# Second mixer's end: all weight subtractions of the output projection on VectorE, and the last two head pairs' softmax scaling too

## The chip, the cores and the metric

The kernel runs on one core of a Trainium2 chip. The time is the device time of one execution in microseconds (us); what is compared is the median of several runs. The engines run side by side, each through its own list of instructions in order: TensorE (PE in the profile, its weight loads PEld) multiplies, VectorE (DVE), ScalarE (ACT) and GpSimd (POOL) do the elementwise work, and SyncE's queue (SP) issues the loads of weights. Engines wait for each other by semaphores.

## The reference, cut to what matters

A decoder trunk of two layers on 256 tokens of width 1024, in float32. Each layer is a half-weighted feed-forward block (SwiGLU, inner width 2816), a token mixer, and a second feed-forward block; the first layer's mixer is a gated DeltaNet, the second layer's is attention in a sliding window with a learned sink per head. The change lies in that second mixer:

```python
def mixer_sliding_window_sinks(h, w_in, b_in, sinks, w_out, b_out):
    ...
    proj = h @ w_in + b_in
    ...
    s = jnp.einsum("bnqhgd,bnkhd->bnhgqk", q, kk).astype(jnp.float32) * (B_HD ** -0.5)
    ...
    p = jax.nn.softmax(jnp.concatenate([s, sink], axis=-1), axis=-1)[..., :-1]
    o = jnp.einsum("bnhgqk,bnkhd->bnqhgd", p.astype(vv.dtype), vv)
    return o.reshape(Bsz, T, HQ) @ w_out + b_out
```

There are 16 query heads of width 64 and 4 key/value heads. The output projection `w_out` is 1024 x 1024.

## The kernel before

**Split operands.** To keep float32's precision on TensorE, each operand is split into a rounded part and a remainder. A weight piece of 512 KB is loaded by SP into a `raw` tile (four buffers), rounded to `whi` by a ScalarE cast (L296), and its remainder `wlo = raw - whi` is made by a subtraction (L297) on VectorE, or on GpSimd where the caller names that engine. A product is then three multiplications (L341 to L343: high x high, high x remainder, remainder x high). A `raw` buffer is free for the next load when its subtraction is done.

**The second mixer, `swa`.** The heads are worked in eight pairs, numbered 0 to 7, each by a generator `attend(j)` whose steps are spread between other work. For a pair TensorE makes the scores (L1152: `psp`, `psc`), VectorE masks them and takes the row maximum (L1162 to L1171), ScalarE takes the exponentials with their row sums (L1176), VectorE adds the sink and takes the reciprocal (L1178, L1179), and one engine multiplies the weights with it (L1180, `att<-att,sl`). After that TensorE transposes them (L1186, `ppt`); ScalarE copies the first token block's part (L1188) and VectorE masks the second's (L1189). The value products follow (L1196, `po`): two for the first token block, which need the copy of L1188, and four for the second, which need L1189. Last, ScalarE casts the result to `oTh` (L1200) and VectorE makes the remainder `oTl` (L1201).

**The output projection.** `out_weights` (L477) loads eight pieces of `w_out`, numbered 0 to 7 here; piece k belongs to pair k. `out` adds a pair's contribution to four accumulators `acc`, in the gaps that `attend` leaves (the list `fill`). In the program's own numbers pieces 4 and 5 are `whi2_8172`/`wlo2_8173`, 6 and 7 are `whi2_8182`/`wlo2_8183`; pair 5's weights are `att_8125`, pair 6's `att_8208`, pair 7's `att_8257`. `po_8241` is pair 4's result, `po_8298` pair 5's, `po_8332` pair 6's. Behind the mixer follows the second feed-forward block, whose first three weight pieces are `raw_8475`, `raw_8482` and `raw_8489`; each is issued by SP as two DMAs of 256 KB (L286), as soon as a `raw` buffer is free, so while the mixer still runs.

**What sets the order.** The kernel is written in one sequence, but the framework's scheduler plans the order on each engine, with its own estimates of durations; a few places are tied by hand with `issue_after`. So a moved instruction shifts its neighbours' places too. Before the change pieces 4 and 6 are subtracted by GpSimd, and all eight pairs' multiplications at L1180 are GpSimd's.

Of the kernel before, what the change touches and what calls it, by code (L numbers as in the profile page):

```python
# [205 lines left out]
class Kern:  # L206
# [894 lines left out]
    def swa(self, nrm, prep, w_in, w_out, after):  # L1101
        nc = self.nc
        bcol, bv, sk, bo = prep
        NP = BH // 2
# [39 lines left out]
        def attend(j):  # L1144
            kv = j // 2
            at = self.big([P, 2048], "att")
            pr = at[:, 0:512].rearrange("p (b h k) -> p b h k", b=NT, h=2)
            pT = at[:, 512:1280].rearrange("p (n h q) -> p n h q", n=3, h=2)
            prv = pr.rearrange("p b h k -> p (b h) k")

            def score(out, b, kt):
                nc.tensor.matmul(out, lhsT=qT[:, j, b * P:(b + 1) * P], rhs=kz[:, kv, :, kt * P:(kt + 1) * P],  # L1152
                                 start=True, stop=True)

            psc, psp = self.psB("psc"), self.psB("psp")
            sc = psc.rearrange("p (b h k) -> p b h k", b=NT, h=2)
            sp = psp[:, 0:256].rearrange("p (h k) -> p h k", h=2)
            score(sp, 1, 0)
            score(sc[:, 1], 1, 1)
            score(sc[:, 0], 0, 0)  # L1160

            nc.vector.copy_predicated(sc[:, 1], self.gt.bitcast(mybir.dt.int32).unsqueeze(1).to_broadcast([P, 2, P]), sp)  # L1162
            nc.vector.tensor_tensor(out=sc[:, 0], in0=sc[:, 0], in1=self.neg.unsqueeze(1).to_broadcast([P, 2, P]),
                                    op=ALU.add)
            m = self.small([P, NT, 2], "smx", 4)
            nc.vector.tensor_reduce(out=m, in_=sc, axis=AX.X, op=ALU.max)
            skb = sk[:, 2 * j:2 * j + 2].unsqueeze(1).to_broadcast([P, NT, 2])
            nc.vector.scalar_tensor_tensor(out=m, in0=m, scalar=HD ** -0.5, in1=skb, op0=ALU.mult, op1=ALU.max)
            es = self.small([P, NT, 2], "ses", 4)
            nc.vector.tensor_tensor(out=es, in0=skb, in1=m, op=ALU.subtract)  # L1170
            nc.vector.tensor_scalar_mul(m, m, -1.0)  # L1171
            nc.scalar.activation(es, es, AF.Exp)
            l = self.small([P, NT, 2], "sl", 4)
            for b in range(NT):
                for i in range(2):
                    nc.scalar.activation(pr[:, b, i, :], sc[:, b, i, :], AF.Exp, scale=HD ** -0.5, bias=m[:, b, i:i + 1],  # L1176
                                         accum_out=l[:, b, i:i + 1])
            nc.vector.tensor_add(l, l, es)  # L1178
            nc.vector.reciprocal(l, l)  # L1179
            nc.gpsimd.tensor_tensor(  # L1180
                out=pr, in0=pr, in1=l.unsqueeze(3).to_broadcast([P, NT, 2, P]), op=ALU.mult)
            yield
            yield
            ps = self.psA("ppt")
            for n in range(4):
                nc.tensor.transpose(ps[:, n * P:(n + 1) * P], prv[:, n, :], self.ident)  # L1186
            pv = ps.rearrange("p (b h q) -> p b h q", b=NT, h=2)
            nc.scalar.copy(pT[:, 0], pv[:, 0])  # L1188
            nc.vector.tensor_tensor(out=pT[:, 1:3], in0=pv[:, 1:2].to_broadcast([P, 2, 2, P]),  # L1189
                                    in1=self.M["st"].unsqueeze(2).to_broadcast([P, 2, 2, P]), op=ALU.mult)  # L1190
            yield
            po = self.psA("po")
            for b in range(NT):
                for i in range(2):
                    for kt in range(b + 1):
                        lastpo[0] = nc.tensor.matmul(po[64 * i:64 * i + 64, b * P:(b + 1) * P],  # L1196
                                         lhsT=v[:, kt, kv * HD:(kv + 1) * HD], rhs=pT[:, b + kt, i, :],
                                         start=kt == 0, stop=kt == b)
            oh = oT_h[:, j, :]
            nc.scalar.copy(oh, po[:, :T])  # L1200
            nc.vector.tensor_sub(oT_l[:, j, :], po[:, :T], oh.bitcast(F32))  # L1201

        lastpo = [None]
        tk.add(attend(0))
        for c in range(1, 4):
            w = self.wcols(w_in, c * 256)
            for f in range(2):
                j = 2 * c + f
                ps = self.psA("pq")
                self.proj_T(ps[:, :T], w, f, nrm)  # L1210
                nc.scalar.activation(qT[:, j, :], ps[:, :T], AF.Identity, bias=bcol[:, j:j + 1])
                tk.tick()
                tk.add(attend(j - 1))
        ws = self.out_weights(w_out, (4, 6))
        tk.tick()
        tk.add(attend(NP - 1))
        oT = [(oT_h[:, :, t * P:(t + 1) * P], oT_l[:, :, t * P:(t + 1) * P]) for t in range(NT)]
        acc = [[ps("acc") for n in range(2)] for ps in (self.psA, self.psB)]
# [109 lines left out]
```

## Time and profile before

| what | value |
|---|---|
| median of 3 runs | 1031.77 us (1029.7 to 1032.34) |
| the profiled execution's own time | 1030.34 us |
| its span, first to last instruction | 1028.6 us |
| mean granted TensorE clock | 0.993 of full speed |
| busy share PE, DVE, ACT, POOL | 98%, 63%, 54%, 24% |
| second mixer's scores to its last value product | 771.7 to 827.5 us of the span |

Times within the span count from its first instruction. A busy share is an average over stages with different limits: what bounds one stage is read from its own stretch of the timeline. In a timeline, a row gives the start, the length, the engine, the line, what it writes and reads, and in brackets the idle time before it and who ended it; neighbouring equal instructions are merged.

### The profile page before, as it was taken

What the parts mean: (1) busy time and instruction counts of PE and PEld (TensorE: products, weight loads), DVE (VectorE), ACT (ScalarE), POOL (GpSimd) and SP (SyncE); (2) the same over time, 40 slices, a digit from 0 to 9 for tenths busy, and PEclk for the clock granted to TensorE, in tenths of its full rate; (3) what the DMA queues carried; (4) which work ended last, traced back from release to release, by engine and by line L of the source; (5) the groups of instructions that cost most, each with busy time, mean ns of one, the idle gap of its engine ahead of it and who ended that gap; (6) DMA issues with size and microseconds to landing.
All of it is one profiled execution on the core that took longest, in us unless ns stands there. A gap on an engine that the chain in (4) does not pass through costs nothing.

```text
span 1028.6 us, 16500 instructions
## 1 busy us (share of the span) xinstructions
PE 1003.0 (98%) x6211; PEld 873.3 (85%) x6211; DVE 649.5 (63%) x967; ACT 552.5 (54%) x1007; POOL 244.8 (24%) x277
## 2 busy tenths in 40 slices
PE   8999999999979999999999999999999999999997
PEld 6888888899878888888888888888898678888886
DVE  6866654666896766666645666664567756666544
ACT  7556543457755646555434555554366645555432
POOL 2233610006744201322200032330021401323100
PEclk9999999999989999999999999999999999999999
DMA  7666666644443335666665666666653426666661
GB/s 250 202 190 186 192 198 196 187 149 127 129 150 90 122 104 164 194 187 193 198 192 182 189 200 187 184 204 193 203 188 120 136 90 205 195 188 192 200 189 42
DMA packets 135252, 177.05 MB, mean 172 GB/s; under 512 B 7186, under 2 KB 120196, under 8 KB 135172
## 3 DMA queue, kind: packets, MB, share of 16 engines
q1 hardware_dynamic: 131968, 171.46, 54.9%
q10 hardware_dynamic: 3204, 4.53, 1.5%
q8 instruction: 49, 0.80, 0.3%
q14 instruction: 31, 0.25, 0.1%
HBM read 174.92 MB, written 1.05 MB: 171 GB/s over the span
## 4 chain that ended last, share of the span: by engine, by line
PE 62%; issue 1%; DVE 1%; ACT 1%; POOLq 0%; POOL 0%; ACTq 0%
PE pg L348 11%; PE pu L348 11%; PE acc L343 7%; PE acc L341 7%; PE acc L342 7%; PE pu L349 6%; PE pg L349 6%; PE pgu L343 1%; PE pgu L342 1%; PE pgu L341 1%; PE pq L341 1%; PE pq L343 1%; PE pq L342 1%; PE psc L1152 1%; PE po L1196 1%
## 5 line engine op out<-in xcount | busy, mean ns | idle before, releaser
L297 DVE TENSOR_TENSOR wlo<-raw,whi 128x1024 fp32r<-128x1024 f32 x302 | 379.9, 1260 | 202.7 <-ACT whi L296 201.7
L296 ACT CAST whi<-raw 128x1024 fp32r<-128x1024 f32 x316 | 330.3, 1052 | 184.8 <-PE acc L343 84.2
L348 PE MATMUL pg<-hs,whi 128*128 128x512 f32 x640 | 225.6, 394 | 0.3 <-DVE hs L203 0.3
L348 PE MATMUL pu<-hs,whi 128*128 128x512 f32 x640 | 225.1, 393 | 0.0
L349 PE MATMUL pu<-hs,wlo 128*128 128x256 f32 x640 | 179.7, 281 | 0.3 <-DVE wlo L297 0.3
L349 PE MATMUL pg<-hs,wlo 128*128 128x256 f32 x640 | 178.9, 280 | 0.0
L348 PEld LDWEIGHTS pg<-hs,whi 128*128 128x128 f32 x640 | 119.9, 187 | 27.7 <-DVE hs L203 0.7
L348 PEld LDWEIGHTS pu<-hs,whi 128*128 128x128 f32 x640 | 119.8, 187 | 27.0
L435 POOL TENSOR_TENSOR act<-act,gate 128x256 f32<-128x256 f32 x80 | 60.2, 752 | 346.5 <-DVE act L434 337.7
L342 PE MATMUL acc<-wlo,ah 128*128 128x512 f32 (+1 forms) x340 | 128.4, 378 | 0.0
L343 PE MATMUL acc<-whi,al 128*128 128x512 f32 (+1 forms) x340 | 128.2, 377 | 0.0
L341 PE MATMUL acc<-whi,ah 128*128 128x512 f32 (+1 forms) x340 | 127.8, 378 | 0.0
L349 PEld LDWEIGHTS pu<-hs,wlo 128*128 128x128 f32 x640 | 120.9, 189 | 0.6 <-DVE wlo L297 0.6
L349 PEld LDWEIGHTS pg<-hs,wlo 128*128 128x128 f32 x640 | 120.9, 189 | 0.4
L341 PEld LDWEIGHTS acc<-whi,ah 128*128 128x128 f32 x340 | 64.0, 188 | 12.0
L342 PEld LDWEIGHTS acc<-wlo,ah 128*128 128x128 f32 x340 | 64.0, 188 | 11.8
L343 PEld LDWEIGHTS acc<-whi,al 128*128 128x128 f32 x340 | 63.9, 188 | 11.9
L438 POOL TENSOR_SCALAR ah<-act 128x256 fp32r<-128x256 f32 x80 | 69.0, 862 | 6.8
L341 PE MATMUL pcv<-hs,whi 128*128 128x256 f32 x192 | 56.5, 294 | 5.9 <-DVE cv L883 5.9
L424 ACT COPY gate<-pg 128x256 f32<-128x256 f32 x80 | 29.5, 369 | 58.9 <-PE pg L349 58.9
L433 ACT COPY act<-pu 128x256 f32<-128x256 f32 x80 | 29.5, 369 | 55.9 <-PE pu L349 55.9
L94 POOL TENSOR_TENSOR rst<-var,mhalf 128x1 f32<-128x1 f32 x10 | 5.6, 557 | 213.7 <-DVE var L92 213.7
(340 smaller groups left out, 1555.7 us busy)
## 6 DMA issues: line engine op xcount, KB each, us to landing
raw<-in_ffn_w_gu_dram SPq DMA_DIRECT2D x160, 512.0 KB, 4.4
raw<-in_ffn_w_down_dram SPq DMA_DIRECT2D x88, 512.0 KB, 4.2
raw<-in_a_w_in_dram SPq DMA_DIRECT2D x32, 512.0 KB, 4.5
raw<-in_ffn_w_gu_dram SPq DMA_DIRECT2D x32, 256.0 KB, 4.7
raw<-in_b_w_in_dram SPq DMA_DIRECT2D x12, 512.0 KB, 4.9
raw<-in_a_w_out_dram SPq DMA_DIRECT2D x8, 512.0 KB, 3.7
raw<-in_b_w_out_dram SPq DMA_DIRECT2D x8, 512.0 KB, 3.7
nw<-in_ffn_norm_dram ACTq DMA_DIRECT2D x3, 512.0 KB, 4.3
```

The costliest lines, as they stand in the source:

```text
L296: nc.scalar.copy(hi, raw)
L297: (eng or nc.vector).tensor_tensor(out=lo, in0=raw, in1=hi.bitcast(F32), op=ALU.subtract)
L341: nc.tensor.matmul(out, lhsT=lh, rhs=rh, start=start, stop=False)
L342: nc.tensor.matmul(out, lhsT=lh, rhs=rl, start=False, stop=False)
L343: return nc.tensor.matmul(out, lhsT=ll, rhs=rh, start=False, stop=stop)
L348: nc.tensor.matmul(out, lhsT=lh, rhs=r2, start=start, stop=False)
L349: return nc.tensor.matmul(out[:, :T], lhsT=ll, rhs=rh, start=False, stop=stop)
L424: nc.scalar.copy(g, pg[:, T:])
L433: nc.scalar.copy(a, pu[:, T:])
L435: nc.gpsimd.tensor_tensor(out=a, in0=a, in1=gates[f], op=ALU.mult)
L438: ahead[2] = nc.gpsimd.tensor_scalar(oh, a, 1.0, None, op0=ALU.mult)
L1152: nc.tensor.matmul(out, lhsT=qT[:, j, b * P:(b + 1) * P], rhs=kz[:, kv, :, kt * P:(kt + 1) * P], start=True, stop=True)
```

## The change

Pieces 4 and 6 of the output projection are no longer given to GpSimd, so all eight subtractions are VectorE's. The multiplication with the reciprocal sums (L1180) goes to VectorE for the last two pairs, 6 and 7; the first six stay on GpSimd.

```diff
@@ -1177,7 +1177,7 @@
                                          accum_out=l[:, b, i:i + 1])
             nc.vector.tensor_add(l, l, es)
             nc.vector.reciprocal(l, l)
-            nc.gpsimd.tensor_tensor(
+            (nc.vector if j >= NP - 2 else nc.gpsimd).tensor_tensor(
                 out=pr, in0=pr, in1=l.unsqueeze(3).to_broadcast([P, NT, 2, P]), op=ALU.mult)
             yield
             yield
@@ -1211,7 +1211,7 @@
                 nc.scalar.activation(qT[:, j, :], ps[:, :T], AF.Identity, bias=bcol[:, j:j + 1])
                 tk.tick()
                 tk.add(attend(j - 1))
-        ws = self.out_weights(w_out, (4, 6))
+        ws = self.out_weights(w_out, ())
         tk.tick()
         tk.add(attend(NP - 1))
         oT = [(oT_h[:, :, t * P:(t + 1) * P], oT_l[:, :, t * P:(t + 1) * P]) for t in range(NT)]
```

GpSimd's list loses these four instructions and is otherwise the same, and so is the sequence of SP's loads. On the other engines the planned order moves. On VectorE, from the masking of pair 7's scores (`psc_8258`), it was:

```order
L1162 COPY_PREDICATED psc_8258<-gt_985,psp_8259 128x256
L1163 TENSOR_TENSOR psc_8258<-psc_8258,neg_988 128x256
L1166 TENSOR_REDUCE smx_8265<-psc_8258 128x4
L297 TENSOR_TENSOR wlo2_8173<-raw_8178,whi2_8172 128x1024
L1201 TENSOR_TENSOR oTl_7762<-po_8192,oTh_7761 128x256
L1168 SCALAR_TENSOR_TENSOR smx_8265<-smx_8265,sk_7535 128x4
L1170 TENSOR_TENSOR ses_8268<-sk_7535,smx_8265 128x4
L1171 TENSOR_SCALAR smx_8265<-smx_8265 128x4
L297 TENSOR_TENSOR wlo2_8183<-raw_8188,whi2_8182 128x1024
L1201 TENSOR_TENSOR oTl_7762<-po_8241,oTh_7761 128x256
```

and is now:

```order
L1162 COPY_PREDICATED psc_8258<-gt_985,psp_8259 128x256
L297 TENSOR_TENSOR wlo2_8173<-raw_8174,whi2_8172 128x1024
L1163 TENSOR_TENSOR psc_8258<-psc_8258,neg_988 128x256
L297 TENSOR_TENSOR wlo2_8173<-raw_8178,whi2_8172 128x1024
L1201 TENSOR_TENSOR oTl_7762<-po_8192,oTh_7761 128x256
L1166 TENSOR_REDUCE smx_8265<-psc_8258 128x4
L297 TENSOR_TENSOR wlo2_8183<-raw_8184,whi2_8182 128x1024
L297 TENSOR_TENSOR wlo2_8183<-raw_8188,whi2_8182 128x1024
L1201 TENSOR_TENSOR oTl_7762<-po_8241,oTh_7761 128x256
L1168 SCALAR_TENSOR_TENSOR smx_8265<-smx_8265,sk_7535 128x4
L1178 TENSOR_TENSOR sl_8223<-sl_8223,ses_8219 128x4
L297 TENSOR_TENSOR wlo_8474<-raw_8475,whi_8473 128x1024
```

The subtractions of pieces 4 (`raw_8174`) and 6 (`raw_8184`) stand before those of 5 and 7, and pair 7's maximum (`smx_8265`) is taken between them; the first subtraction for the next block (`wlo_8474`) stands ahead of pair 5's L1189, no longer behind it.

A little later on VectorE, from pair 5's L1189 on, it was:

```order
L1189 TENSOR_TENSOR att_8125<-ppt_8250,sufftri_956 128x512
L297 TENSOR_TENSOR wlo_8474<-raw_8475,whi_8473 128x1024
L297 TENSOR_TENSOR wlo_8481<-raw_8482,whi_8480 128x1024
L1201 TENSOR_TENSOR oTl_7762<-po_8298,oTh_7761 128x256
L1189 TENSOR_TENSOR att_8208<-ppt_8307,sufftri_956 128x512
L297 TENSOR_TENSOR wlo_8488<-raw_8489,whi_8487 128x1024
```

and is now:

```order
L1189 TENSOR_TENSOR att_8125<-ppt_8250,sufftri_956 128x512
L1170 TENSOR_TENSOR ses_8268<-sk_7535,smx_8265 128x4
L1179 RECIPROCAL sl_8223<-sl_8223 128x4
L297 TENSOR_TENSOR wlo_8481<-raw_8482,whi_8480 128x1024
L1171 TENSOR_SCALAR smx_8265<-smx_8265 128x4
L1180 TENSOR_TENSOR att_8208<-att_8208,sl_8223 128x512
L1201 TENSOR_TENSOR oTl_7762<-po_8298,oTh_7761 128x256
L1178 TENSOR_TENSOR sl_8272<-sl_8272,ses_8268 128x4
L1179 RECIPROCAL sl_8272<-sl_8272 128x4
L1180 TENSOR_TENSOR att_8257<-att_8257,sl_8272 128x512
L297 TENSOR_TENSOR wlo_8488<-raw_8489,whi_8487 128x1024
L1189 TENSOR_TENSOR att_8208<-ppt_8307,sufftri_956 128x512
```

The two multiplications at L1180 (`att_8208`, `att_8257`) are new here, and the third subtraction for the next block (`wlo_8488`) now stands before pair 6's L1189 (`att_8208<-ppt_8307`), where it stood behind it.

On ScalarE, from the cast of pair 4's result, it was:

```order
L1200 CAST oTh_7761<-po_8241 128x256
L1176 ACTIVATE att_8208,sl_8223<-psc_8209,smx_8216 128x128 x4
L1172 ACTIVATE ses_8268<-ses_8268 128x4
L1176 ACTIVATE att_8257,sl_8272<-psc_8258,smx_8265 128x128 x4
L1188 COPY att_8125<-ppt_8250 128x256
L296 CAST whi_8473<-raw_8475 128x1024
L296 CAST whi_8480<-raw_8482 128x1024
L1200 CAST oTh_7761<-po_8298 128x256
L1188 COPY att_8208<-ppt_8307 128x256
L296 CAST whi_8487<-raw_8489 128x1024
```

and is now:

```order
L1200 CAST oTh_7761<-po_8241 128x256
L1176 ACTIVATE att_8208,sl_8223<-psc_8209,smx_8216 128x128 x4
L296 CAST whi_8473<-raw_8475 128x1024
L1188 COPY att_8125<-ppt_8250 128x256
L296 CAST whi_8480<-raw_8482 128x1024
L1172 ACTIVATE ses_8268<-ses_8268 128x4
L1200 CAST oTh_7761<-po_8298 128x256
L1176 ACTIVATE att_8257,sl_8272<-psc_8258,smx_8265 128x128 x4
L296 CAST whi_8487<-raw_8489 128x1024
L1188 COPY att_8208<-ppt_8307 128x256
```

The casts for the next block (`whi_8473`, `whi_8480`, `whi_8487`) each moved ahead of work for the pairs: the first ahead of pair 5's copy (`att_8125<-ppt_8250`), the second ahead of pair 7's exponentials (`att_8257,sl_8272`), the third ahead of pair 6's copy (`att_8208<-ppt_8307`). On TensorE, pair 5's first two value products moved ahead of the L343 multiplications with piece 4, and pair 6's transposes behind pair 5's contribution to the projection.

## Rows read from the trace of the kernel before

**Rows 1.** The page's busy time by engine: us, share of the span, number of instructions.
```profile
PE 1003.0 (98%) x6211; PEld 873.3 (85%) x6211; DVE 649.5 (63%) x967; ACT 552.5 (54%) x1007; POOL 244.8 (24%) x277
```

**Rows 2.** From the chain of waits that ended last, narrowed to the end of the second mixer: start in us, length in us, engine, what it writes, line.
```profile
808.53 2.39 DVE wlo L297
...
811.25 1.95 DVE smx L1168
```

**Rows 3.** TensorE's timeline at the same place: start, length, line, operands, count; in brackets the idle time before it and who ended it.
```profile
813.11 0.40 PE L342 MATMUL acc<-wlo,oTh 128*128 128x512 f32 x1
815.15 0.73 PE L343 MATMUL acc<-whi,oTl 128*128 128x512 f32 x2 [1.64 <-DVE oTl L1201]
...
820.05 0.39 PE L343 MATMUL acc<-whi,oTl 128*128 128x512 f32 x1
820.28 0.40 PE L341 MATMUL acc<-whi,oTh 128*128 128x512 f32 x1
...
821.30 0.44 PE L1196 MATMUL po<-att,v 128*64 128x128 f32 x4
821.67 0.73 PE L343 MATMUL acc<-whi,oTl 128*128 128x512 f32 x2
822.34 0.66 PE L1196 MATMUL po<-att,v 128*64 128x128 f32 x8
822.93 0.66 PE L1186 MATMUL ppt<-ident,att 128*128 128x128 f32 x4
823.34 0.48 PE L341 MATMUL acc<-whi,oTh 128*128 128x512 f32 x1
```

**Rows 4.** Stretches of the span: length, then busy us (and instructions) of PE, PEld, DVE, ACT and POOL, the granted TensorE clock, the DMA engines' share and their GB/s.
```profile
813.50:815.20 1.70, 0.06 (x2) 0.05 (x1) 1.67 (x5) 1.70 (x10) 0.00 (x0) 1.00 0.92 286
815.20:816.20 1.00, 1.00 (x6) 0.44 (x6) 0.97 (x4) 1.00 (x2) 0.65 (x1) 1.00 0.74 256
816.20:819.70 3.50, 3.47 (x18) 2.79 (x17) 2.59 (x4) 1.73 (x4) 2.37 (x2) 0.51 0.90 269
819.70:822.50 2.80, 2.80 (x17) 1.68 (x17) 1.83 (x3) 1.05 (x1) 0.00 (x0) 1.00 0.95 309
```

**Rows 5.** VectorE's timeline from the masking of pair 7's scores on.
```profile
806.99 0.43 DVE L1162 COPY_PREDICATED psc<-gt,psp 128x256 f32<-128x256 int32 x1 [0.72 <-PE psc L1152]
807.45 0.43 DVE L1163 TENSOR_TENSOR psc<-psc,neg 128x256 f32<-128x256 f32 x1
807.92 0.69 DVE L1166 TENSOR_REDUCE smx<-psc 128x4 f32<-128x512 f32 x1
808.53 2.39 DVE L297 TENSOR_TENSOR wlo<-raw,whi 128x1024 fp32r<-128x1024 f32 x1
...
811.18 2.01 DVE L1168 SCALAR_TENSOR_TENSOR smx<-smx,sk 128x4 f32<-128x4 f32 x1
...
813.53 1.23 DVE L297 TENSOR_TENSOR wlo<-raw,whi 128x1024 fp32r<-128x1024 f32 x1
814.68 0.42 DVE L1201 TENSOR_TENSOR oTl<-po,oTh 128x256 fp32r<-128x256 f32 x1
```

**Rows 6.** GpSimd's timeline, its two weight pieces.
```profile
807.43 2.40 POOL L297 TENSOR_TENSOR wlo<-raw,whi 128x1024 fp32r<-128x1024 f32 x1
...
809.79 3.38 POOL L297 TENSOR_TENSOR wlo<-raw,whi 128x1024 fp32r<-128x1024 f32 x1
```

**Rows 7.** Durations: the page's costliest groups (busy us, mean ns of one, idle time before them), and for L1189 on VectorE the smallest, median and largest ns.
```profile
L297 DVE TENSOR_TENSOR wlo<-raw,whi 128x1024 fp32r<-128x1024 f32 x302 | 379.9, 1260 | 202.7 <-ACT whi L296 201.7
L296 ACT CAST whi<-raw 128x1024 fp32r<-128x1024 f32 x316 | 330.3, 1052 | 184.8 <-PE acc L343 84.2
...
L1189 DVE TENSOR_TENSOR att<-ppt,sufftri x8: 660/686/692, 784.0 to 824.0; 128x512 f32<-128x512 f32 x8
```

**Rows 8.** SP's timeline, the loads for the next block (start, length of the issue), and the time from issue to landing of the eight DMAs of L286 there.
```profile
810.95 0.56 SPq L286 DMA_DIRECT2D raw<-in_ffn_w_gu_dram  x1
...
811.56 0.61 SPq L286 DMA_DIRECT2D raw<-in_ffn_w_gu_dram  x1
...
812.26 1.22 SPq L286 DMA_DIRECT2D raw<-in_ffn_w_gu_dram  x2
...
DMA to landing us min/median/max: 3.2/4.4/4.5
```

**Rows 9.** ScalarE's timeline: pair 7's first exponential, pair 5's copy behind the last one, and the cast of the next block's second piece.
```profile
813.63 0.37 ACT L1176 ACTIVATE att<-psc,smx 128x128 f32<-128x128 f32 x1
...
815.01 0.38 ACT L1188 COPY att<-ppt 128x256 f32<-128x256 f32 x1
...
817.35 1.05 ACT L296 CAST whi<-raw 128x1024 fp32r<-128x1024 f32 x1 [1.01 <-DMA raw<-in_ffn_w_gu_dram]
```

**Rows 10.** Stretches with other waits of TensorE, each with the one behind it, and the stretch before the next block's loads; columns as in rows 4.
```profile
7.00:11.40 4.40, 2.29 (x16) 1.78 (x14) 2.58 (x5) 2.68 (x4) 0.00 (x0) 1.00 0.97 323
11.40:15.00 3.60, 3.49 (x14) 2.57 (x15) 3.29 (x4) 2.50 (x4) 0.00 (x0) 1.00 1.07 370
355.00:358.60 3.60, 2.05 (x11) 1.39 (x10) 2.06 (x7) 2.58 (x15) 1.33 (x2) 1.00 1.04 343
358.60:362.20 3.60, 2.98 (x25) 2.75 (x26) 1.91 (x8) 1.40 (x8) 0.69 (x1) 1.00 0.34 121
807.50:810.00 2.50, 2.50 (x20) 2.02 (x19) 2.46 (x3) 2.50 (x6) 2.50 (x2) 1.00 0.00 0
```

## The prediction

> **What bounds the kernel now.** I read the page's busy shares first. TensorE is busy 98% of the span and VectorE 63% [rows 1], so a change on VectorE and GpSimd can pay only where TensorE stands still. Then the chain of waits, narrowed to the end of the second mixer: there it leaves TensorE once for long, and from 808.5 us on runs over VectorE, with a weight piece's subtraction of 2.39 us and a tiny 128x4 operation of 1.95 us [rows 2]. TensorE's timeline shows the price: its last multiplication before starts at 813.11, the next, an L343 with piece 4, at 815.15, with 1.64 us idle put down to VectorE's oTl [rows 3]. The stretches show a second price: the granted clock is 1.00 (the 2.4 GHz level) during that idle time, and 0.51 (the 1.2 GHz level) from 816.2 to 819.7 [rows 4].
>
> VectorE's and GpSimd's timelines say why. GpSimd subtracts pieces 4 and 6 from 807.43 to 809.8 and from 809.79 to 813.2 [rows 6]. VectorE's subtraction that starts meanwhile takes 2.39 us, where the mean of 302 is 1.26, and its 128x4 operation takes 2.01 us and ends at 813.19, when GpSimd's second piece does [rows 5 to 7]. So each engine waits until the other's running instruction is over. GpSimd suffers too: 3.38 us for its second piece against 2.40 for its first [rows 6]. Without GpSimd's two pieces VectorE has 1.16 + 1.86 = 3.0 us less to stand.
>
> **The change part by part.** VectorE receives two subtractions at 1.23 and two 128x512 multiplications. The latter are in no VectorE row; half a subtraction is 0.62 and L1189, as large but with one PSUM operand, takes 0.69, so I take 0.69, between 0.6 and 1.23 [rows 5, 7]. That is 2 x 1.23 + 2 x 0.69 = 3.8 us added against 3.0 us returned. VectorE thus gets 0.8 us longer in all, but not evenly, and the order of the engines decides, so I walk it with row durations.
>
> VectorE's first part gets shorter. Copy_predicated starts at 806.99 as before [rows 5]; the four subtractions follow with L1163 (0.43), L1201 (0.42) and L1166 (0.68) between: piece 4 ends at 808.6, piece 5 at 810.1 (was 810.9), pieces 6 and 7 at 812.2 and 813.4 (was 814.8), and pair 4's oTl at 813.7, where it was 815.1. The stall of rows 3 would be nearly gone: TensorE could go on at 813.11 + 0.23 = 813.35.
>
> The planned order puts other waits there. ScalarE now casts the next block's first weight piece ahead of pair 5's L1188 copy, and TensorE takes pair 5's first value products, which need that copy, ahead of the L343 pair. The cast needs its load. SP issues it when piece 4's buffer is free, at 808.6 and 809.2 (issues are 0.6 apart), where it was at 810.95 [rows 8]. Landing takes 3.2 to 4.5 us [rows 8]; with the queues empty I take 3.2, so the load lands at 812.5. The cast (1.05) ends at 813.55, the copy (0.38) at 813.95 [rows 7, 9]. TensorE waits 0.6 us.
>
> Then two value products (0.37) and the L343 pair run until about 814.8 [rows 3]. The other four value products need L1189 on VectorE, which stands behind the subtraction of that new piece: 813.55 + 1.23 + 0.69 = 815.5. TensorE waits another 0.6 us, then runs 0.59 for the products, ten multiplications at 0.23, the transposes at 0.5 and the L343 pair at 0.46: it is through at 819.45 [rows 3].
>
> Pair 6 is next. The block's second piece is issued at 810.1 and 810.7; the cast of that load waited for it until 817.35, after a last issue at 812.9, so 4.4 us: it lands at 815.1 [rows 8, 9]. Cast until 816.15, VectorE's subtraction until 817.4, and only behind it the small L1171 (817.55), on which pair 7's four exponentials wait; these take 1.4 us [rows 9], until 819.0. The third piece's cast follows until 820.05 and then pair 6's copy until 820.4: TensorE waits 0.95 us. Its last four products need pair 6's L1189, behind the third piece's subtraction, which starts after pair 7's multiplication at about 820.25: 820.25 + 1.15 + 0.69 = 822.1. That is a further wait of 1.3 us.
>
> In the kernel before, those four products of pair 6 start at 822.34 [rows 3], after 1.64 us of idle time and about half of 3.4 us, 1.7 us, lost to the lower clock [rows 4]. After the change they start at 822.1, after 0.6 + 0.6 + 0.95 + 1.3 = 3.45 us of shorter waits and no fall of the clock. From there on the order of all engines is the same. The sum is -0.25 us: what is gained is nearly all handed to casts and subtractions that the plan moved ahead of TensorE's operands.
>
> What is sized worst is the second load's landing. At 3.2 us the walk ends 0.7 us earlier (-1.0); with 0.8 us more of queueing it ends at +0.5. The multiplication at 0.6 or 1.23 moves the end by -0.1 to +0.5, since one of them stands on the path. That the loads start 2.3 us earlier costs nothing: the DMA engines stand idle from 807.5 to 810 [rows 10], and nothing else is loaded then.
>
> Taking work away from GpSimd goes against one page. The Trainium skill, "Perfetto Trace Analysis", section "Optimizing Scalar/DVE Operations", says that some work may be offloaded, even to GpSimd, if VectorE is saturated, and adds that the shared port may make this useless. VectorE is busy 1.67 of 1.70 us in the stall [rows 4], so the first half would put the moved work, 3.8 us, on the end; the second half fits the rows better, since 3.0 us of that busy time is waiting.
>
> **The rivals.**
>
> A, slower: the new waits bring the low clock again. They lie at 819.45 to 822.1, 2.25 us idle of 2.65, with TensorE full behind them. Then 3.4 us run at the 1.2 GHz level and 1.7 us are lost with nothing to hide them: -0.25 + 1.7 = +1.45. For it: 1.64 us of idle time was followed by the fall [rows 3, 4]. Against it: from 7.00 to 11.40 TensorE was idle for 2.1 of 4.4 us, and from 355.00 to 358.60 for 1.55 of 3.6 us, and the clock stayed at 1.00 then and behind [rows 10]. [...]
>
> B, faster: the casts come earlier than I walk, for instance because both loads land in 3.2 us and ScalarE takes them in its own gaps, and TensorE does not wait. Then the whole price returns: -1.64 - 1.7 = -3.35. For it, VectorE's first part is 1.4 us earlier. Against it, four separate waits would have to go.
>
> C, VectorE becomes the bound: the 0.8 us by which its work exceeds the returned waits lies wholly on the end, +0.8. For it, TensorE's last wait ends on VectorE in my walk. Against it, VectorE is busy for only 2.59 of 3.5 and 1.83 of 2.8 us in the next stretches [rows 4]. The change does what it says: GpSimd's list loses exactly the four instructions.
>
> **How the numbers follow.** The profiled execution took 1030.34 us with a span of 1028.6; the median of three runs is 1031.77, 1.43 us more, and the runs spread over 2.6 us. On the profiled one: forecast 1030.1, A 1031.8, B 1027.0, C 1031.1. On the median: forecast 1031.5 (its own range, -1.0 to +0.5, 1030.8 to 1032.3), A 1033.2, B 1028.4, C 1032.6. Chances: forecast 0.54, A 0.22, C 0.14, B 0.10. Some 1.3 us of run spread goes on either side, so 1029.2 to 1033.7 holds eight in ten: B is left out, A's centre is in. A measurement of this kernel can tell about 0.3%, 3.1 us: below 1028.7 lies about half of B and a little of the forecast's spread, above 1034.9 only the far part of A and C. That gives faster 0.09, same 0.83, slower 0.08.
>
> **What would show it.** Right: VectorE's subtractions of 1.23 us throughout, no 128x4 operation above 0.2 us; pair 4's oTl near 813.7; the first load issued near 808.6; TensorE waits put down to att L1188 and L1189 around 814, 815, 820 and 822, of 0.5 to 1.3 us. Wrong: a granted clock of 0.5 after 822 (A); no TensorE wait above 0.5 us between 813 and 823 (B); VectorE without gaps from 813 to 824 (C). A subtraction that stays at 2.4 us with GpSimd idle would overturn the reading of the stall.

## The result, and the profile after

The changed kernel took 1033.39 us in the median of 20 runs (1029.26 to 1035.3), the kernel before 1030.52 us in the median of 20 runs beside it. The ratio is 1.0020, with a 95% interval of 1.0012 to 1.0029: slower by 2.1 us (1.2 to 3.0). The medians lie further apart, 2.9 us, because 12 of the changed kernel's 20 runs lie above 1033 us and the rest at 1029 to 1032; the means are 2.0 us apart. That is within the 0.3% named in the prediction, but the interval leaves out zero, and the forecast had the other sign (-0.25 us). That the median lies in the range of 1029.2 to 1033.7 is luck: the range was laid around a median of three runs of the kernel before, 1031.77, which 20 runs put at 1030.52. Moved by that 1.25 us it would have ended at 1032.5.

The profiled execution took 1033.9 us, with a span of 1032.2. The page's busy time by engine of the changed kernel answers to [rows 1]: VectorE has the same sum with four more instructions, GpSimd 8.9 us less with four fewer.

```profile
PE 1004.0 (97%) x6211; PEld 875.2 (85%) x6211; DVE 649.5 (63%) x971; ACT 552.4 (54%) x1007; POOL 235.9 (23%) x273
```

In the profiled execution the masking of pair 7's scores, with which the prediction's walk begins, starts at 810.75, where it was 806.99. Up to there every engine runs the same instructions in the same order in both programs. Two stretches of some 3.4 us each at half the clock, so about 3.4 us lost in all, account for nearly all of the 3.76 us; the profile of the kernel before has 1.00 in both. Stretches of the changed kernel, columns as in [rows 4]:

```profile
12.70:16.20 3.50, 3.50 (x10) 2.44 (x9) 2.97 (x3) 2.85 (x6) 0.00 (x0) 0.51 1.06 365
313.10:316.50 3.40, 3.40 (x26) 3.38 (x17) 3.26 (x10) 1.22 (x2) 0.33 (x1) 0.50 0.55 155
```

So places are compared with 3.76 taken off. VectorE's timeline of the changed kernel, from that masking on, answers to [rows 5]:

```profile
810.75 0.43 DVE L1162 COPY_PREDICATED psc<-gt,psp 128x256 f32<-128x256 int32 x1 [0.72 <-PE psc L1152]
811.08 1.23 DVE L297 TENSOR_TENSOR wlo<-raw,whi 128x1024 fp32r<-128x1024 f32 x1
...
814.64 2.34 DVE L297 TENSOR_TENSOR wlo<-raw,whi 128x1024 fp32r<-128x1024 f32 x2
816.90 0.41 DVE L1201 TENSOR_TENSOR oTl<-po,oTh 128x256 fp32r<-128x256 f32 x1
817.24 0.15 DVE L1168 SCALAR_TENSOR_TENSOR smx<-smx,sk 128x4 f32<-128x4 f32 x1
...
817.38 1.22 DVE L297 TENSOR_TENSOR wlo<-raw,whi 128x1024 fp32r<-128x1024 f32 x1
818.51 0.68 DVE L1189 TENSOR_TENSOR att<-ppt,sufftri 128x512 f32<-128x512 f32 x1
...
823.01 0.69 DVE L1180 TENSOR_TENSOR att<-att,sl 128x512 f32<-128x512 f32 x1
823.63 1.22 DVE L297 TENSOR_TENSOR wlo<-raw,whi 128x1024 fp32r<-128x1024 f32 x1
824.76 0.68 DVE L1189 TENSOR_TENSOR att<-ppt,sufftri 128x512 f32<-128x512 f32 x1
```

Every subtraction now takes 1.2 us, the 128x4 operation of L1168 0.15 (was 2.01), the moved multiplication 0.69. Pair 4's `oTl` ends at 817.31, that is 813.55 in the old count. But the subtraction at 817.38 belongs to the next block, and pair 5's masking (L1189) stands behind it; the one at 823.63 stands in the same way before pair 6's masking. On ScalarE the casts stand before the copies (L1188), and the first waits for its load; ScalarE's timeline of the changed kernel:

```profile
816.20 1.05 ACT L296 CAST whi<-raw 128x1024 fp32r<-128x1024 f32 x1 [0.83 <-DMA raw<-in_ffn_w_gu_dram]
817.15 0.36 ACT L1188 COPY att<-ppt 128x256 f32<-128x256 f32 x1
...
822.45 1.06 ACT L296 CAST whi<-raw 128x1024 fp32r<-128x1024 f32 x1
823.39 0.39 ACT L1188 COPY att<-ppt 128x256 f32<-128x256 f32 x1
```

TensorE's timeline of the changed kernel shows what that costs, where [rows 3] had one idle time of 1.64 us:

```profile
817.57 0.44 PE L1196 MATMUL po<-att,v 128*64 128x128 f32 x4 [0.31 <-ACT att L1188]
...
819.25 0.67 PE L1196 MATMUL po<-att,v 128*64 128x128 f32 x8 [0.58 <-DVE att L1189]
...
823.83 0.44 PE L1196 MATMUL po<-att,v 128*64 128x128 f32 x4 [0.52 <-ACT att L1188]
...
825.50 0.66 PE L1196 MATMUL po<-att,v 128*64 128x128 f32 x8 [1.22 <-DVE att L1189]
```

Four waits, 0.31 + 0.58 + 0.52 + 1.22 = 2.63 us, each put down to the copy or the masking of the pair whose products wait. The clock stays at its 2.4 GHz level through all of it, as the stretches of the changed kernel show (against 0.51 from 816.2 to 819.7 in [rows 4]):

```profile
816.20:819.70 3.50, 2.61 (x19) 1.45 (x17) 3.15 (x8) 2.36 (x4) 0.00 (x0) 1.00 0.90 245
...
822.50:824.00 1.50, 0.98 (x9) 0.55 (x8) 1.32 (x4) 1.28 (x3) 0.00 (x0) 1.00 1.09 376
824.00:826.00 2.00, 0.78 (x12) 0.45 (x10) 1.44 (x2) 0.00 (x0) 0.00 (x0) 1.00 0.33 116
```

The place itself is thus no longer than before. From the start of pair 7's masking (L1162) to the first residual addition behind the mixer (L491) it takes 832.63 - 810.75 = 21.88 us, where it took 829.46 - 806.99 = 22.47. What made this execution 3.56 us longer is the 3.76 us of earlier low clock, less 0.59, plus 0.4 us at the very end of the program. That does not explain a change that is slower in the median: one pair of profiles cannot tell it, and so the place was read in every run below.

### The profile page after: what moved, and what is told of

It reads as the page before. It is cut to its first block, busy times and chain, and to the rows that moved or that the text cites. A ratio compares the mean times of both kernels' runs of the same rounds, so it can differ in the third digit from the quotient of the medians.

```text
span 1032.2 us, 16495 instructions
## 1 busy us (share of the span) xinstructions
PE 1004.0 (97%) x6211; PEld 875.2 (85%) x6211; DVE 649.5 (63%) x971; ACT 552.4 (54%) x1007; POOL 235.9 (23%) x273
## 4 chain that ended last, share of the span: by engine, by line
PE 61%; ACT 1%; issue 1%; DVE 1%; DMA 0%; POOLq 0%; POOL 0%; SPq 0%; ACTq 0%
PE pg L348 11%; PE pu L348 11%; PE acc L341 7%; PE acc L342 7%; PE acc L343 7%; PE pu L349 6%; PE pg L349 6%; PE pgu L343 1%; PE pgu L342 1%; PE pgu L341 1%; PE pq L341 1%; PE pq L343 1%; PE pq L342 1%; PE psc L1152 1%; PE po L1196 0%
## 5 line engine op out<-in xcount | busy, mean ns | idle before, releaser
L343 PE MATMUL acc<-whi,al 128*128 128x512 f32 (+1 forms) x340 | 128.4, 378 | 0.0
L343 PEld LDWEIGHTS acc<-whi,al 128*128 128x128 f32 x340 | 64.0, 188 | 11.9
```

The costliest lines, as they stand in the source:

```text
L343: return nc.tensor.matmul(out, lhsT=ll, rhs=rh, start=False, stop=stop)
```

## The experiments

Theory 1: the loss is the order in which casts and subtractions for the next block stand before pair 5's and 6's operands. Theory 2: it is the clock, or spread between executions. Theory 3: it is the two multiplications that VectorE took over. Two lengths of each profile are compared, both from the start of L1162 for pair 7: "to the products", the start of pair 6's last four value products, and "to the addition", the start of the first residual addition. The waits are those of TensorE up to the products; one of 0.48 us behind them stands in every run and is left out. "Closing" is from the last output DMA's issue to the end of the span.

| run | to the products | to the addition | low clock before the addition | TensorE's waits up to the products | closing |
|---|---|---|---|---|---|
| before | 15.35 | 22.47 | yes | 1.64 | 3.5 |
| e0_null | 14.17 | 21.29 | no | 1.64, 0.29 | 3.5 |
| e3_mults | 16.16 | 23.27 | yes | 1.65, 0.84 | 3.5 |
| after | 14.75 | 21.88 | no | 0.31, 0.58, 0.52, 1.22 | 3.9 |
| e6_again | 14.55 | 23.26 | yes | 0.29, 0.60, 0.34, 1.22 | 3.9 |
| e9_again2 | 14.47 | 21.61 | no | 0.37, 0.52, 0.20, 1.22 | 3.9 |
| e2_subs | 15.95 | 24.67 | yes | 0.39, 0.51, 1.21, 1.73 | 3.5 |
| e10_hold_third | 13.44 | 20.57 | no | 0.55, 0.49, 0.29 | 3.9 |
| e5_hold7 | 12.06 | 19.18 | no | 0.21 | 3.9 |
| e7_subs_hold7 | 12.04 | 19.16 | no | 0.21 | 3.5 |
| e11_gp5 | 12.03 | 19.17 | no | 0.21 | 3.5 |
| e8_before_hold7 | 13.82 | 20.95 | no | 1.64 | 3.5 |

**The kernel before, once more** (no edit).

> The kernel before once more, to see it in another execution. S is the stretch from VectorE's masking of pair 7's scores (L1162) to the start of pair 6's last four value products; S was 15.35 us in the profile before, with a fall of the clock inside, and 14.75 us after, with none. Theory 1 (the fall is not in every execution, and I charged it as if it were): where the profile shows the clock at 1.00 all through, S is 15.35 - 1.7 = 13.65 us; with the fall it is 15.35 again. Theory 2 (S is always 15.35 before, the change gains 0.6 us there, and the 2 us come from earlier stretches by chance): S is 15.35, and its times against the kernel before spread as far as the change's did, with medians 1 to 2 us apart. Theory 1 has the time within 0.7 us of before.

Measured: 1030.57 us against 1030.61, ratio 0.9998 (0.9986 to 1.0010). The same wait of 1.64 us is there, but the clock does not fall behind it. TensorE's timeline and the stretch behind the wait, e0_null:

```profile
816.66 0.73 PE L343 MATMUL acc<-whi,oTl 128*128 128x512 f32 x2 [1.64 <-DVE oTl L1201]
...
821.64 0.44 PE L1196 MATMUL po<-att,v 128*64 128x128 f32 x4 [0.29 <-DVE oTl L1201]
```

```profile
817.70:821.20 3.50, 3.47 (x24) 2.62 (x22) 2.89 (x4) 2.19 (x5) 2.38 (x2) 1.00 0.92 285
```

What follows: the same instructions, with the same wait, run at 0.51 in one execution and at 1.00 in another. The fall costs 22.47 - 21.29 = 1.2 us between these two, not 1.7: without it TensorE reaches pair 6's first products 0.29 us too early and waits there. So the length to the products, 14.17 us, lies between the 13.65 of theory 1 and the 15.35 of theory 2.

**Only the subtractions moved.** The multiplications of the last two pairs stay on GpSimd; the edit against the changed kernel:

```diff
-            (nc.vector if j >= NP - 2 else nc.gpsimd).tensor_tensor(
+            nc.gpsimd.tensor_tensor(
```

> The subtractions of pieces 4 and 6 on VectorE, the last two pairs' multiplications still on GpSimd. The planned order of casts and copies is that of the whole change. Theory 1 (the waits that this order makes are the loss): TensorE waits of 0.3, 0.6, 0.5 and 1.1 us as after the change, S about 14.7 us without a fall, time 0.8 to 2 us over before. Theory 3 (the added multiplications on VectorE are the loss): the last wait is 0.7 us shorter, S about 14.0, time as before within 0.5 us.

Measured: 1035.12 us, ratio 1.0042 (1.0028 to 1.0055), 2.3 us above the whole change in the same measure. Neither theory had that: the first had 0.8 to 2 us, the third as before within 0.5. The planned order is that of the change, and now GpSimd's multiplications meet VectorE's subtractions. GpSimd's, VectorE's and TensorE's timelines of e2_subs:

```profile
816.28 1.04 POOL L1180 TENSOR_TENSOR att<-att,sl 128x512 f32<-128x512 f32 x1 [8.29 <-DVE sl L1179]
820.67 1.04 POOL L1180 TENSOR_TENSOR att<-att,sl 128x512 f32<-128x512 f32 x1 [3.35 <-DVE sl L1179]
```

```profile
816.43 1.98 DVE L297 TENSOR_TENSOR wlo<-raw,whi 128x1024 fp32r<-128x1024 f32 x1 [0.32 <-ACT whi L296]
...
820.99 1.80 DVE L297 TENSOR_TENSOR wlo<-raw,whi 128x1024 fp32r<-128x1024 f32 x1 [0.49 <-ACT whi L296]
```

```profile
821.28 0.44 PE L1196 MATMUL po<-att,v 128*64 128x128 f32 x4 [1.21 <-ACT att L1188]
...
823.45 0.67 PE L1196 MATMUL po<-att,v 128*64 128x128 f32 x8 [1.73 <-DVE att L1189]
```

Each subtraction that starts while GpSimd multiplies ends about 1.1 us after GpSimd (817.32 and 821.71), as if it had started only then. The delay runs on through L1171, pair 7's exponentials and the third cast to pair 6's operands. So in this order the moved multiplications are not the loss: they spare it some 2 us.

**Only the multiplications moved.** Pieces 4 and 6 stay on GpSimd; the edit against the kernel before:

```diff
-            nc.gpsimd.tensor_tensor(
+            (nc.vector if j >= NP - 2 else nc.gpsimd).tensor_tensor(
```

> The last two pairs' multiplications on VectorE, pieces 4 and 6 still subtracted on GpSimd. The planned order of casts stays that of before. Theory 1: the old wait of 1.64 us stays, one multiplication of 0.69 us stands ahead of pair 5's L1189 and TensorE waits 0.6 us for it, S 0.6 us over before, time +0.3 to +0.9 us. Theory 3: this alone gives the whole loss, +2 us.

Measured: 1032.53 us, ratio 1.0013 (1.0002 to 1.0025). The old stall stays, and a wait is added, because pair 6's multiplication now stands on VectorE before pair 5's masking. TensorE's timeline of e3_mults:

```profile
814.69 0.73 PE L343 MATMUL acc<-whi,oTl 128*128 128x512 f32 x2 [1.65 <-DVE oTl L1201]
...
816.63 1.12 PE L1196 MATMUL po<-att,v 128*64 128x128 f32 x8 [0.84 <-DVE att L1189]
```

Against the profile of before, which also has the fall, the place is 23.27 - 22.47 = 0.8 us longer. The one multiplication ahead of pair 5's masking takes 0.69 us of that. The time is a little above the 0.3 to 0.9 us of theory 1.

**The change with the order mended.** The cast and the subtraction of the next block's first three pieces are queued behind pair 7's copy and masking, by the framework's tie on the order of issue; nothing else is edited:

```diff
+            if self.pair is not None:
+                for ins in self.pair[1:]:
+                    behind.enter_context(self.tc.issue_after(ins.ins))
...
-            nc.scalar.copy(pT[:, 0], pv[:, 0])
-            nc.vector.tensor_tensor(out=pT[:, 1:3], in0=pv[:, 1:2].to_broadcast([P, 2, 2, P]),
+            cp = nc.scalar.copy(pT[:, 0], pv[:, 0])
+            mk = nc.vector.tensor_tensor(out=pT[:, 1:3], in0=pv[:, 1:2].to_broadcast([P, 2, 2, P]),
...
+            if j == NP - 1:
+                self.pair = [3, cp, mk]
```

> The whole change, and the first three casts and subtractions for the next block are queued behind pair 7's copy (ScalarE) and masking (VectorE). Theory 1: with the order mended, none of the four waits stays above 0.4 us, S about 11.8 us, no fall there, time 2 to 3 us under before. Theory 2: the order is worth at most the 2.6 us of waits in one execution in which the earlier stretches are kind, and the time against before is within 1 us. If the loads for the next block then come too late, TensorE waits in that block's first weight piece instead, around 838 us.

Measured: 1027.94 us against 1030.61, ratio 0.9979 (0.9968 to 0.9989), 2.2 us faster than before and some 4 us faster than the change. TensorE's timeline of e5_hold7 (line numbers are 7 to 9 higher at this place) has no wait above 0.21 us before pair 5's and pair 6's products, and VectorE's has the maskings ahead of the next block's subtractions:

```profile
814.19 0.44 PE L1205 MATMUL po<-att,v 128*64 128x128 f32 x4 [0.21 <-DVE sl L1185]
...
815.22 0.67 PE L1205 MATMUL po<-att,v 128*64 128x128 f32 x8
...
819.26 0.93 PE L1205 MATMUL po<-att,v 128*64 128x128 f32 x12
```

```profile
814.10 0.68 DVE L1196 TENSOR_TENSOR att<-ppt,sufftri 128x512 f32<-128x512 f32 x1
...
818.38 0.69 DVE L1196 TENSOR_TENSOR att<-ppt,sufftri 128x512 f32<-128x512 f32 x1 [0.46 <-ACT att L1195]
...
822.16 2.36 DVE L304 TENSOR_TENSOR wlo<-raw,whi 128x1024 fp32r<-128x1024 f32 x2 [0.26 <-ACT whi L303]
```

The order alone turns the sign of the change: with the same work on the same engines the place takes 19.18 us in place of 21.6 to 21.9. The next block is not held up by it: from the first residual addition to the end it takes 199.55 us, as after the change (199.54).

**The change twice more** (no edit): e6_again in twelve runs, e9_again2 in a single profiled run, beside the two kernels that follow.

> The whole change once more, for its local price in another execution. S2 is the stretch from VectorE's masking of pair 7's scores to the first residual addition (L491); so far 21.3 us in the kernel before without a fall of the clock, 22.5 with one, 21.9 after the change without. Theory 1 (the new waits cost 1 us more than the old one, and when the clock falls it falls behind them, where nothing hides it): S2 is 21.9 us again, or 23.4 to 23.8 with a fall; time 1 to 3 us over before. Theory 2 (the 2 us were chance in earlier stretches): S2 is 21.9 or less, and the time is within 0.7 us of before.

> The whole change a third time, one look. Theory 1: S2 is 21.9 us without a fall of the clock in the stretch or just behind it, 23.4 to 23.8 with one; TensorE's waits are again 0.3, 0.6, 0.5 and 1.2 us, since their order is set by the program. A wait that differs by over 0.3 us between these looks would come from the landing of the loads.

Measured: e6_again 1032.05 us against 1030.41, ratio 1.0015 (1.0006 to 1.0024); e9_again2 1031.66 us, a single run. The loss comes back. In e6_again the clock falls right behind the last two waits, in the other two profiles of the change it does not. TensorE's timeline and the stretch behind the waits, e6_again:

```profile
822.02 0.67 PE L1196 MATMUL po<-att,v 128*64 128x128 f32 x8 [1.22 <-DVE att L1189]
822.62 0.78 PE L1186 MATMUL ppt<-ident,att 128*128 128x128 f32 x4
```

```profile
822.90:826.50 3.60, 3.60 (x12) 2.92 (x11) 1.12 (x2) 0.59 (x2) 0.00 (x0) 0.53 0.38 130
```

That fall costs 23.26 against 21.61 to 21.88, so 1.4 to 1.7 us (23.4 to 23.8 in all had been expected), with no new wait behind it to take any of it back. The wait before pair 6's first products is 0.52 us after the change, 0.34 in e6_again and 0.20 in e9_again2. That follows the landing of the second piece's load: ScalarE's cast of it, which waits for the load, starts 7.90, 7.70 and 7.62 us behind the masking of pair 7's scores.

**Only the subtractions moved, order mended.** All eight multiplications stay on GpSimd; the edit against e5_hold7:

```diff
-            (nc.vector if j >= NP - 2 else nc.gpsimd).tensor_tensor(
+            nc.gpsimd.tensor_tensor(
```

> All subtractions on VectorE, all multiplications with the reciprocal sums left on GpSimd, and the next block's first three casts and subtractions queued behind pair 7's copy and masking. If the moved multiplications matter only through what stands ahead of them: S2 19.2 to 19.6 us as with the whole change in this order, time 2 to 3 us under before. If GpSimd's multiplications are themselves too slow or block VectorE: a TensorE wait of 0.5 to 1.5 us at pair 6's or 7's transposes, S2 20 us or more.

Measured: 1027.60 us, ratio 0.9973 (0.9957 to 0.9989), the place 19.16 us as in e5_hold7. Once the subtractions of the next block are out of the way, it does not matter to the place which engine multiplies for the last two pairs.

**The order alone, on the kernel before.** Pieces 4 and 6 are on GpSimd again; the edit against e7_subs_hold7:

```diff
-        ws = self.out_weights(w_out, ())
+        ws = self.out_weights(w_out, (4, 6))
```

> The kernel before, with only the queueing of the next block's first three casts and subtractions behind pair 7's copy and masking. Nothing of the change is in it. Theory 1: the old wait of 1.64 us for pair 4's oTl stays, S2 21.0 to 22.5 us, time within 0.7 us of before: the queueing alone is worth nothing. Rival: the queueing alone gives the 2 us that the change with it gave.

Measured: 1029.71 us against 1030.41, ratio 0.9996 (0.9988 to 1.0005): nothing that can be told from none. The wait of 1.64 us is still there, and the place takes 20.95 us, just below the 21.0 to 22.5 expected. So the gain needs both the subtractions on VectorE, which take the wait away, and the order, which keeps new ones out.

**One piece put back.** The change with only the third piece's cast and subtraction queued behind pair 7's copy and masking, so that they no longer stand before pair 6's; the edit against e5_hold7:

```diff
-                for ins in self.pair[1:]:
+                for ins in self.pair[1:] if self.pair[0] == 1 else []:
```

> The change as it is, with one piece put back: only the cast and the subtraction of the next block's third weight piece are queued behind pair 7's copy and masking, so that they stand behind pair 6's copy (L1188) and masking (L1189) again; nothing else on any engine's list moves. Theory 1 (the loss is the order, piece by piece): the waits before pair 6's value products, 0.52 and 1.22 us, go, those before pair 5's, 0.31 and 0.58 us, stay; from the masking of pair 7's scores to pair 6's last four products 12.7 to 13.1 us, where the change takes 14.5 to 14.8 without a fall of the clock and the wholly mended order 12.06. Time 1.3 to 1.7 us below the change: ratio 0.998 to 1.000. A rival (the waits replace each other: TensorE is only as early as VectorE's whole load allows): a wait of about 1.5 us shows up at pair 6's masking all the same, and the stretch stays above 14 us.

Measured: 1030.03 us against 1030.54, ratio 0.9999 (0.9976 to 1.0021); 13.44 us to the products, 0.3 more than was expected. The interval of the times is too wide to set this kernel apart from the change (1.0015 and 1.0020), so the reading rests on the profile. VectorE's and TensorE's timelines of e10_hold_third:

```profile
822.10 0.69 DVE L1187 TENSOR_TENSOR att<-att,sl 128x512 f32<-128x512 f32 x1
822.85 0.69 DVE L1196 TENSOR_TENSOR att<-ppt,sufftri 128x512 f32<-128x512 f32 x1
```

```profile
823.60 0.66 PE L1205 MATMUL po<-att,v 128*64 128x128 f32 x8 [0.29 <-DVE att L1196]
```

The waits of 0.52 and 1.22 us are gone but for 0.29, which comes from pair 7's multiplication standing before pair 6's masking; those before pair 5's products stay. The third piece is worth 1.0 to 1.3 us of the place, the first two another 1.4 (13.44 - 12.06): in these profiles the loss is made piece by piece, and a wait that is taken away does not come back elsewhere in full.

**The closing.** The mended order with five memsets of 128x4, which nothing reads, put by the planner near the head of GpSimd's list, about 1.5 us into the span; the edit against e5_hold7:

```diff
+                zz = self.small([P, 4], "zz", 1)
+                for _ in range(5):
+                    nc.gpsimd.memset(zz, 0.0)
```

> The whole change with the mended order, as in e5_hold7, and five idle memsets of 128x4 at the head of GpSimd's list, which bring it back to its old length. If the 0.4 us that every run with the whole change needs more in its closing (199.54 to 199.57 us from the first residual addition behind the mixer to the end, where runs with GpSimd's longer list need 199.13 to 199.15) hang on the length of GpSimd's list, they go: 199.14 us. If they hang on which engine multiplies for the last two pairs, they stay: 199.55 us. The stretch from the masking of pair 7's scores to pair 6's last four products stays at 12.1 us under either.

Measured: 1030.83 us in a single run, too few to compare times; the place takes 19.17 us, as in e5_hold7. The closing falls back to its old length. The last output DMA's issue in ScalarE's queue, in the timelines of before, e5_hold7 and e11_gp5; their spans end at 1028.6, 1026.2 and 1029.1:

```profile
1025.10 0.35 ACTq L138 DMA_DIRECT2D out_dram<-xw  x1
```

```profile
1022.29 0.35 ACTq L138 DMA_DIRECT2D out_dram<-xw  x1
```

```profile
1025.62 0.35 ACTq L138 DMA_DIRECT2D out_dram<-xw  x1
```

That is 3.5, 3.9 and 3.5 us. So the last 0.4 us hang on the length of GpSimd's list (or on where its end falls), and not on the engine that multiplies. For e11_gp5 that is a single run; the eleven other profiles agree, with 3.9 us in the five of programs with the shortest list and 3.5 in the six others.

## Why the prediction was right or wrong

**The stall: right.** With GpSimd idle every subtraction takes 1.2 us and L1168 0.15; pair 4's `oTl` ends at 813.55 in the old count, where 813.7 was walked. The 3.0 us that VectorE stood in the kernel before were waiting for GpSimd, and e2_subs shows it again with other instructions. The prediction misplaced them in one sentence: they are not part of the 1.67 busy us of the stall [rows 4], but lie ahead of it, from 808.5 to 813.2 [rows 5]. "Perfetto Trace Analysis", the page of the Trainium skill that was weighed, would have spoken against the change by its advice to offload and for it by its warning of the shared port; here the warning decides, as e7_subs_hold7 shows: with the order mended, taking the two subtractions away from GpSimd gains 2.8 us, although VectorE is busy nearly throughout the stall.

**The walk behind it: right in its mechanism, and slightly too long.** SP issues the next block's first load at 812.34, in the old count 808.58, where 808.6 was walked:

```profile
812.34 6.04 SPq L286 DMA_DIRECT2D raw<-in_ffn_w_gu_dram  x8
```

The four waits fell where they were said to, on the operands named, at 0.31, 0.58, 0.52 and 1.22 us where 0.6, 0.6, 0.95 and 1.3 were walked. Pair 6's last four products start at 821.74 in the old count, where 822.1 was walked. The multiplication at 0.69 was right to the digit. The second wait is 0.7 by the walk's own times (815.5 - 814.8), and the sum does not agree with itself: the starts give 822.1 - 822.34 = -0.24, but the prices named beside it give 3.45 - 1.64 - 1.7 = +0.1.

**The step that failed: the price of the old stall.** The prediction put against the new waits "1.64 us of idle time and about half of 3.4 us, 1.7 us, lost to the lower clock", and so came to -0.25. The 1.7 us were read from one profile and booked as if each execution paid them. The runs show the fall behind that same wait in two profiles of four (before and e3_mults, but not e0_null and e8_before_hold7), and a net price of 1.2 us where it comes. The new order has the fall in two profiles of four as well (e6_again and e2_subs, not after and e9_again2), at 1.4 to 1.7 us in e6_again. So the clock is on both sides of the sum and nearly cancels. The granted clocks of all runs say the same from more executions: their mean is 0.9929 in the 32 runs of the change and 0.9928 in the 78 runs of the kernel before that were taken beside the experiments. One fall more or less in every run, 3.4 us at half the clock, would show as 0.0017. On average the change takes no fall away, and the loss is not made of more falls either. What is left of the sum are the waits: 2.63 us after (2.31 in e9_again2) against 1.64 + 0.29 in e0_null, 0.4 to 0.7 us more. Like against like the place says the same: without a fall 21.61 and 21.88 against 21.29, with it 23.26 against 22.47, so 0.3 to 0.8 us longer. Had the sum been made without the clock, on the same walk, it would have read -0.25 + 1.7 = +1.45, or +0.9 at the fall's measured price of 1.2 us: the right sign either way.

**A term that was missing: the closing**, 0.4 us more in every profile of the whole change but e11_gp5, whose list was made longer. Together with the 0.3 to 0.8 us of the place that is 0.7 to 1.2 us. The two measurements of the change say 1.2 to 3.0 and 0.6 to 2.5 us. The sum lies within the second interval and only touches the first, so up to 1 us or so may be left without a cause. The stretches ahead of the place, the same in all these programs (e11_gp5 has only its memsets there), put its start anywhere from 806.5 to 810.8 us, and with a handful of profiles nothing smaller than that spread can be read there.

**The rivals.** A, the low clock brought by the new waits, did happen, at the place and nearly at the price given (1.4 to 1.7 against 1.7 us), but only in some executions, and the length of the waits does not sort them: after, with 1.74 us of idle time in the two waits before pair 6's products, kept its clock, and e6_again, with 1.56, lost it. What the prediction held against A, two waits behind which the clock stayed at 1.00 [rows 10], was again the reading of one execution. In e9_again2 the same two waits are longer, 3.3 of 4.4 us and, a little later in the span, 2.0 of 3.6 us idle, and the clock falls behind both; stretches of e9_again2, columns as there:

```profile
7.00:11.40 4.40, 1.08 (x7) 0.57 (x5) 2.53 (x5) 2.63 (x4) 0.00 (x0) 1.00 0.98 326
11.40:15.00 3.60, 3.53 (x9) 2.75 (x10) 3.29 (x5) 2.49 (x4) 0.00 (x0) 0.53 1.07 370
...
356.00:359.60 3.60, 1.60 (x10) 1.08 (x9) 2.06 (x9) 2.16 (x12) 1.81 (x2) 1.00 0.97 315
359.60:363.20 3.60, 3.60 (x20) 3.60 (x19) 1.27 (x5) 0.67 (x5) 0.20 (x1) 0.53 0.17 60
```

B, no waits, did not happen by itself; e5_hold7 brings it about, and its -2.2 us is less than the -3.35 given because the clock's 1.7 were counted in there too. C, VectorE as the bound, fell: in e5_hold7 VectorE does the same work, three pieces of it later, and TensorE doesn't wait. That the change does what it says was right.

**The cost by part.** The subtractions alone, in the planned order, +4.3 us (1.0042); the multiplications alone +1.3 (1.0013); both +2.1 and +1.6 in two measurements; both with the order mended -2.2; the subtractions with the order mended -2.8; the order alone nothing. So a gain was there to be had, and the planner's placing of three casts and three subtractions more than gave it back.

## What to carry to other kernels

When a change frees an engine, look at what the planner moves into the gap: work for the next stage that comes a little early costs little by its own length, and much by standing in order before an operand that TensorE waits for; tie it behind that operand, and measure the move and the order apart. A price that is read from one profiled execution, a fall of the clock above all, is first looked for in a second profile of the same kernel before it enters a sum.

## What the runs showed of the hardware

- The granted clock after one and the same wait of TensorE (1.64 us, same instructions around it) was 0.51 in one execution and 1.00 in another. The Trainium skill, "TensorE: Matmul & The Clock Gate", section "What's actually happening", says of the rise at a kernel's start that its place varies from run to run; the profiles go further, since the fall came or did not come at all.
- A VectorE subtraction that starts 0.15 to 0.32 us after a GpSimd multiplication of 1.04 us takes 1.98 and 1.80 us in place of 1.23: it loses most of what is left of GpSimd's instruction, 0.75 of 0.89 us and 0.57 of 0.72, as if it had hardly begun before GpSimd was done. The Trainium skill, "SBUF — State Buffer", section "SBUF: two separate sides", calls the two engines' shared ports an exclusive lock held for the whole instruction; e2_subs and [rows 5, 6] agree.
- The program's closing was 0.4 us longer with GpSimd's list a few instructions shorter (3.9 against 3.5 us), and five idle memsets took that away. What in the list's end makes it was not tried. The Trainium skill, "Runtime: NRT & Kernel Launch", section "Instruction fetch mechanics", says that an engine's instructions are fetched in blocks; whether a block's end plays a part here no run shows.
